# A two-layer decoder on one core: W1 units set between the K tile pairs of the pass before, and every middle pair taken by seven products

## Chip, cores and metric

The kernel runs on one core of one Trainium2 chip. The metric is device time in microseconds of one execution, as the median over several runs. Everything is float32 at the interface; TensorE works on float32 values that are cut into a high and a low part (fp32r), three matmuls for each product.

## The reference, cut to what matters

256 tokens of width 2048 go through two layers. Layer 0 is a gated short convolution, layer 1 is latent attention; each is followed by a DeepNorm and by the same kind of MLP, which is the part that the change touches:

```python
def sq_relu_mlp(x, w1, w2):
    return jnp.square(jax.nn.relu(x @ w1)) @ w2
...
h = layer_norm(ALPHA * h + sq_relu_mlp(h, mlp_w1[layer], mlp_w2[layer]),
               ln_g[layer, 1], ln_b[layer, 1])
```

w1 is 2048 by 8192 and w2 is 8192 by 2048, for each of the two layers.

## The kernel before, in words

**Passes and units.** The hidden width 8192 is cut into NQ = 8 passes of QC = 8 chunks of 128 columns. In pass q each chunk is one *W1 unit*: 16 K tiles of the input, and for each a 512-wide matmul with the high part of the weights over the high and low parts of the 256 tokens (`high`, L215) and a 256-wide one with the low part of the weights (`low`, L219), into one PSUM bank (`mm_run`, `products`). A unit is then evacuated (`whole`, L355 and L356), goes through Relu and Square on ScalarE (L718, L719), and is cut into high and low parts. The 256 columns of two neighbouring chunks and the matching rows of w2 make a *K tile pair* of the second product.

**The second product.** Pass 0 and pass 7 use plain `down`. The six passes between (`FAST`) add to running sums. In each, the four output blocks of 512 columns are taken as two groups g of two blocks. A pair can be taken *by seven products* (Strassen's scheme in Winograd's form, `fast_products`): sums and differences of the four activation quarters (S1 to S4, made by `form`) and of the four weight quarters (T1 to T4, made on the fly in `prepare`) give seven 128 by 128 by 512 products in place of eight. Each product is a `dot`, three 512-wide matmuls (L300, L302, L303). The seven running sums live in seven PSUM banks while they are added to; between uses they are parked in SBUF (in `acc` and `sums`) by copies on ScalarE. `MIXED = "sssp"` says that group 1 takes three pairs by seven products and the fourth pair plainly, by eight dots; group 0 takes all four by seven. One dot of the plain pair (`EVEN`) has its middle matmul cut in two.

**Order of the work.** In a middle pass the eight W1 units come first, back to back, on four banks in turn (`busy`); `resume` brings the parked sums of group 1 back while they run. Then `down_pairs` takes the four pairs of group 1, parks its sums, brings back those of group 0, takes its four pairs and parks or adds those. The first unit of a stretch has its third K tile `TURNED`: low before high.

**Weights.** All weights come in one `stream` in the order of use, 512 KB a load, through SyncE's DMA queue into RAW = 5 raw buffers. `prepare` cuts each into high (ScalarE cast, L127) and low (VectorE subtraction, L128); a pair for seven products is two loads and adds L162, L166, L169 and a third and a fourth cut. There are WA = 8 buffers each for high and low parts. `take` hands out the next prepared weights and emits the preparation of those up to LOOK = 5 pieces further on. The order on each engine's queue is fixed when the program is built, by the order in which the instructions are emitted and by when they are expected to be ready.

**Other work beside.** In pass 7 of the first MLP, `begin` subtracts a mean from the 16 chunks of the residual for the next norm; in passes 1 to 4 of the second MLP, `extra` adds the turned residual to one block each; in pass 7 `fold` adds the seven sums together, for both groups at once with 1024-wide VectorE instructions (L676).

Of the kernel before, what the change touches and what calls it, by code (L numbers as in the profile page):

```python
# [10 lines left out]
F32 = mybir.dt.float32  # L11
# [5 lines left out]
P = 128  # L17
# [5 lines left out]
NQ = 8  # L23
# [14 lines left out]
MIXED = "sssp"  # L38
EVEN = (QC - 1, "22")
# [14 lines left out]
def trunk(ctx: ExitStack, tc: tile.TileContext, xT, vecs, lead, w_first, w_in, w_out, w_kv, w_q, w_uk, w_uv,  # L54
# [27 lines left out]

    def mlp_stream(l):
        out = []
        for q in range(NQ):
            out += halves(w1[l, q * QC:(q + 1) * QC])
            if q not in FAST:
                out += halves(w2[l, q])
                continue
            for j, kind in enumerate(MIXED):  # L90
                out += [(w2f[l, q, 1, j, 0], w2f[l, q, 1, j, 1])] if kind == "s" else \
                    halves(w2[l, q, 2, j]) + halves(w2[l, q, 3, j])
            out += [(w2f[l, q, 0, j, 0], w2f[l, q, 0, j, 1]) for j in range(QC // 2)]
        return out
# [210 lines left out]
    def held(x, t):  # L305

        return [x[:, o + t * P:o + (t + 1) * P] for o in (0, T)]
# [35 lines left out]
    def fast_products(ps, x, forms, j, fresh, ready, onto=()):  # L343

        b, = take(1)
        a = {"11": held(x[2 * j], 0), "12": held(x[2 * j + 1], 0), "22": held(x[2 * j + 1], 1)}
        for i in range(4):
            a[f"S{i + 1}"] = [forms[:, j, o, i * P:(i + 1) * P] for o in range(2)]
        for p, l, r in FACTORS:
            dot(ps[p], b[r], a[l], p in fresh, p in ready, onto=p in onto)  # L350
# [224 lines left out]
    def mlp(idx, ln, blocks, fast, begin=None, extra=None, last=False):  # L575
# [27 lines left out]
        def place(p, g):  # L603

            return sums[:, OWN.index(p), g, :] if p in OWN else \
                block(*{"2": (2 * g, 0), "3": (2 * g + 1, 0), "4": (2 * g, 1), "22": (2 * g + 1, 1)}[p])

        def resumed(p, g, name, bank):

            ps = psum(name, bank)  # L610
            if q != FAST[0] or p not in OWN:
                nc.scalar.copy(ps, place(p, g))
            return ps
# [4 lines left out]
        def keep(p, g, ps):  # L618

            at = place(p, g)  # L620
            if q == FAST[0] and p in OWN:
                nc.scalar.copy(at, ps)
            else:
                nc.vector.tensor_tensor(at, at, ps, ALU.add)

        def resume(busy, free, ps, m):

            b2, b3, b4, b6 = free
            b1, b5, b7, b22 = busy
            for p, bank in {3: (("3", b3),), 4: (("2", b2),), 5: (("4", b4), ("1", b1)), 6: (("6", b6), ("5", b5)),  # L630
                            7: (("7", b7), ("22", b22))}.get(m, ()):
                ps[p] = resumed(p, 1, f"ps_r{p}", bank)

        def down_pairs(h, forms, busy, free, ps):

            b2, b3, b4, b6 = free
            b1, b5, b7, b22 = busy
            new = set(OWN) if q == FAST[0] else set()
            onto = set(ps) - new
            for j, kind in enumerate(MIXED):  # L640
                if kind == "s":
                    last = j == MIXED.rindex("s")
                    fast_products(ps, h, forms, j, new if j == 0 else (), OWN if last else (), onto)
                    if last:
                        for p in OWN:
                            put_back(p, 1, ps[p])
                        then = {p: resumed(p, 0, f"ps_f{p}", bank) for p, bank in (("3", b1), ("1", b5))}
                    continue
                for two in (((0, "2"), (1, "4")), ((1, "22"), (0, "3"))):
                    w, = take(1, LOOK + 1)  # L650
                    for t, p in two:
                        for kk in range(2):
                            k = 2 * j + kk
                            dot(ps[p], wide_rows(w, kk), held(h[k], t), False, k == QC - 1, (k, p) == EVEN, True)
                    if j == len(MIXED) - 1:
                        if "5" not in then:
                            then.update({p: resumed(p, 0, f"ps_f{p}", bank) for p, bank in (("5", b7), ("7", b6))})
                        for _, p in two:
                            put_back(p, 1, ps[p])
            n = QC // 2  # L660
            onto = set(then) - new
            then.update({p: psum(f"ps_f{p}", bank) for p, bank in (("2", b2), ("6", b4), ("4", b22))})
            for j in range(n):
                fast_products(then, h, forms, j, set(then) - onto if j == 0 else (), then if j == n - 1 else (), onto)
            for p, _, _ in FACTORS:
                (put_back if p in onto or p in new else keep)(p, 0, then[p])
            return (b3, b1, b5, b7), (b6, b2, b4, b22)

        def fold():

            s1, s5, s7, s6 = (sums[:, i] for i in range(4))
            c = acc.rearrange("p t (g b c) -> p t b g c", g=2, b=2)
            for d, a, b in ((c[:, 0, 0], c[:, 0, 0], s1), (s6, s6, s1), (c[:, 0, 1], c[:, 0, 1], s6), (s7, s7, s6),
                            (c[:, 1, 0], c[:, 1, 0], s7), (c[:, 1, 1], c[:, 1, 1], s7),
                            (c[:, 0, 1], c[:, 0, 1], s5), (c[:, 1, 1], c[:, 1, 1], s5)):
                nc.vector.tensor_tensor(d, a, b, ALU.add)  # L676
                yield
# [8 lines left out]
        busy, free = (0, 1, 2, 3), (4, 5, 6, 7)  # L686
        for q in range(NQ):
            ht = act.tile([P, QC, 2 * T], F32R, tag="c", name=f"h{idx}_{q}")
            h = [ht[:, k, :] for k in range(QC)]
            forms = None  # L690
            if q in FAST:
                forms = act.tile([P, QC // 2, 2, 4 * P], F32R, tag="a2", name=f"forms{idx}_{q}")
            pair = []

            def pair_tile(m):

                if m % 2 == 0:
                    pool = (act, "ab") if m % 4 else (fast, "fp")
                    t = pool[0].tile([P, 2 * T], F32, tag=pool[1], name="fp")
                    pair.append(t.rearrange("p (i t) -> p i t", i=2))  # L700
                return pair[-1]

            def form(j):
                (a11, a21), (a12, a22) = ((pair[j][:, i, :P], pair[j][:, i, P:]) for i in range(2))
                sf = fast.tile([P, 4, P], F32, tag="sf", name="sf")
                s1, s2, s3, s4 = (sf[:, i, :] for i in range(4))
                nc.vector.tensor_tensor(s1, a21, a22, ALU.add)
                nc.vector.tensor_tensor(s3, a21, a11, ALU.subtract)
                nc.vector.tensor_tensor(s2, s1, a11, ALU.subtract)
                nc.vector.tensor_tensor(s4, a12, s2, ALU.subtract)  # L710
                split(forms[:, j, 0, :], forms[:, j, 1, :], sf.rearrange("p i c -> p (i c)"))

            def hidden(m, ps, evac, *func):
                both = pair_tile(m) if q in FAST else None
                f = both[:, m % 2, :] if both is not None else tmp.tile([P, T], F32, tag="fh", name="fh", bufs=3)
                evac(ps, f, *func)
                if not func:
                    nc.scalar.activation(f, f, AF.Relu)  # L718
                nc.scalar.activation(f, f, AF.Square)  # L719
                if both is None:  # L720
                    put_split(h[m], f)
                elif m % 2:
                    at = ht[:, m - 1:m + 1, :]
                    split(at[:, :, :T], at[:, :, T:], both)
                    form(m // 2)

            if q == 0:
                for m in range(QC):
                    if m < GROUP:
                        if m == 0:  # L730
                            ws = ln.ws if ln.ws else group_of(GROUP)
                            if not ln.ws:
                                mm_wide(ws, ln.xd)
                            ln.finish()
                        ps = ws[m][1]
                    else:
                        ws = [(take(), psum("ps_w"))]
                        mm_wide(ws, ln.xd)
                        ps = ws[0][1]
                    hidden(m, ps, ln.weighted, AF.Relu)  # L740
                acc = act.tile([P, 2, D], F32, tag="a1", name=f"acc{idx}")
            else:
                folds = fold()
                begun = {}
                for m, ps in enumerate(products(QC, xhl, TURNED, busy)):
                    hidden(m, ps, whole)
                    if extra and m == 0 and q <= NB:
                        for t in range(2):
                            extra(block, q - 1, t, busy[2 + t])
# [438 lines left out]
```

## Time and profile before

| what | value |
|---|---|
| median of 3 runs (lowest, highest) | 2000.58 us (2000.33, 2001.18) |
| the profiled execution's span, first to last instruction | 1994.9 us |
| around it: the median less this span | 5.7 us |
| granted TensorE clock, mean | 1.000 |
| DMA, mean over the span | 193 GB/s |

The profile is of one execution. It gives no time for that execution beside its span, so the last row sets the span against the median of the runs; a forecast is made on the span and carried over with that difference. The span is measured from the first to the last instruction. [...]

### The profile page before, as it was taken

What the parts mean: (1) busy time and instruction counts of PE and PEld (TensorE: products, weight loads), DVE (VectorE), ACT (ScalarE), POOL (GpSimd) and SP (SyncE); (2) the same over time, 40 slices, a digit from 0 to 9 for tenths busy, and PEclk for the clock granted to TensorE, in tenths of its full rate; (3) what the DMA queues carried; (4) which work ended last, traced back from release to release, by engine and by line L of the source; (5) the groups of instructions that cost most, each with busy time, mean ns of one, the idle gap of its engine ahead of it and who ended that gap; (6) DMA issues with size and microseconds to landing.
All of it is one profiled execution on the core that took longest, in us unless ns stands there. A gap on an engine that the chain in (4) does not pass through costs nothing.

```text
span 1994.9 us, 30180 instructions
## 1 busy us (share of the span) xinstructions
PE 1987.7 (100%) x11110; PEld 1737.2 (87%) x11110; DVE 1709.4 (86%) x2555; ACT 1354.9 (68%) x2154; POOL 2.3 (0%) x21
## 2 busy tenths in 40 slices
PE   9999999999999999999999999999999999999998
PEld 8888888988888888888889998898888888888886
DVE  8667667797999989989978988777899999999985
ACT  6444445586778778777756755558677787887772
POOL 0000000000000000000000000000000000000000
PEclk9999999999999999999999999999999999999999
DMA  8666666565657466574855543656464656656483
GB/s 318 205 191 187 190 190 190 179 193 157 212 170 251 148 216 221 177 243 147 281 171 159 170 140 123 201 180 195 146 233 155 232 161 220 222 178 233 150 269 130
DMA packets 106853, 385.85 MB, mean 193 GB/s; under 512 B 11857, under 2 KB 12625, under 8 KB 106449
## 3 DMA queue, kind: packets, MB, share of 16 engines
q1 hardware_dynamic: 106560, 383.79, 59.5%
q8 instruction: 87, 1.43, 0.3%
q14 instruction: 62, 0.50, 0.1%
q10 hardware_dynamic: 144, 0.13, 0.0%
HBM read 381.78 MB, written 2.10 MB: 192 GB/s over the span
## 4 chain that ended last, share of the span: by engine, by line
PE 98%; DVE 1%; ACT 1%; issue 0%; DVEq 0%; ACTq 0%
PE ps_u L215 20%; PE ps_l L215 13%; PE ps_u L219 10%; PE ps_l L219 7%; PE ps_f L300 4%; PE ps_f L303 4%; PE ps_f L302 4%; PE ps_r L303 4%; PE ps_r L302 4%; PE ps_r L300 4%; PE ps_d L300 2%; PE ps_d L302 2%; PE ps_d L303 2%; PE ps_w L249 2%; PE ps_w L248 2%; PE ps_w L247 2%
## 5 line engine op out<-in xcount | busy, mean ns | idle before, releaser
L128 DVE TENSOR_TENSOR lo<-raw,hi 128x1024 fp32r<-128x1024 f32 x710 | 861.8, 1220 | 190.6 <-ACT hi L127 119.9
L127 ACT CAST hi<-raw 128x1024 fp32r<-128x1024 f32 x710 | 741.8, 1051 | 247.4 <-PE ps_l L215 98.1
L215 PE MATMUL ps_u<-xhl,hi 128*128 128x512 f32 x1792 | 621.7, 392 | 0.0
L219 PE MATMUL ps_u<-xhl,lo 128*128 128x256 f32 x1792 | 498.2, 279 | 0.0
L215 PEld LDWEIGHTS ps_u<-xhl,hi 128*128 128x128 f32 x1792 | 334.5, 187 | 73.6 <-ACT acc L595 0.2
L219 PEld LDWEIGHTS ps_u<-xhl,lo 128*128 128x128 f32 x1792 | 338.1, 189 | 1.8
L215 PE MATMUL ps_l<-xhl_a,hi 128*128 128x512 f32 x704 | 244.1, 393 | 0.0
L219 PE MATMUL ps_l<-xhl_a,lo 128*128 128x256 f32 x704 | 195.4, 279 | 0.0
L215 PEld LDWEIGHTS ps_l<-xhl_a,hi 128*128 128x128 f32 x704 | 132.1, 188 | 29.9
L219 PEld LDWEIGHTS ps_l<-xhl_a,lo 128*128 128x128 f32 x704 | 131.9, 188 | 0.2
L127 ACT CAST hi_t<-raw_t 128x1024 fp32r<-128x1024 f32 x84 | 88.5, 1054 | 45.8 <-DVE raw_t L162 41.4
L162 DVE TENSOR_TENSOR raw_t<-raw,raw 128x1024 f32<-128x1024 f32 x84 | 102.3, 1218 | 1.8 <-DMA raw<-in_w2f_dram 1.5
L128 DVE TENSOR_TENSOR lo_t<-raw_t,hi_t 128x1024 fp32r<-128x1024 f32 x84 | 102.4, 1219 | 0.2
L718 ACT ACTIVATE fp<-fp 128x256 f32<-128x256 f32 x96 | 40.0, 416 | 63.2 <-DVE fp L356 62.6
L215 PE MATMUL ps_l<-z,hi 128*128 128x512 f32 x240 | 82.4, 391 | 0.0
L300 PE MATMUL ps_d<-hi,h 128*128 128x512 f32 x192 | 75.0, 391 | 0.0
L302 PE MATMUL ps_d<-lo,h 128*128 128x512 f32 x192 | 75.0, 390 | 0.0
L303 PE MATMUL ps_d<-hi,h 128*128 128x512 f32 x192 | 74.8, 389 | 0.0
L249 PE MATMUL ps_w<-xd,hi 128*128 128x258 f32 x256 | 72.7, 284 | 0.0
L248 PE MATMUL ps_w<-xd,lo 128*128 128x258 f32 x256 | 72.3, 282 | 0.0
L247 PE MATMUL ps_w<-xd,hi 128*128 128x258 f32 x256 | 72.3, 282 | 0.0
L215 PE MATMUL ps_l<-oT,hi 128*128 128x512 f32 x208 | 71.3, 391 | 0.0
(296 smaller groups left out, 3963.7 us busy)
## 6 DMA issues: line engine op xcount, KB each, us to landing
raw<-in_w_dram SPq DMA_DIRECT2D x344, 512.0 KB, 4.5
raw<-in_w2f_dram SPq DMA_DIRECT2D x168, 512.0 KB, 3.9
raw<-in_w_in_dram SPq DMA_DIRECT2D x88, 512.0 KB, 4.2
raw<-in_w_out_dram SPq DMA_DIRECT2D x32, 512.0 KB, 3.7
raw<-in_w_o_dram SPq DMA_DIRECT2D x32, 512.0 KB, 4.2
raw<-in_w_kv_dram SPq DMA_DIRECT2D x10, 512.0 KB, 3.7
raw<-in_w_q_dram SPq DMA_DIRECT2D x8, 512.0 KB, 4.0
raw<-in_w_uk_dram SPq DMA_DIRECT2D x8, 512.0 KB, 3.9
```

The costliest lines, as they stand in the source:

```text
L127: nc.scalar.copy(hi, src)
L128: nc.vector.tensor_tensor(lo, src, hi.bitcast(F32), ALU.subtract)
L162: nc.vector.tensor_tensor(t.rearrange(two, a=2), b12.unsqueeze(1).to_broadcast([P, 2, BW]), r1.rearrange(two, a=2), ALU.subtract)
L215: nc.tensor.matmul(ps, w[blk // 8][0][:, blk % 8, :], x, start=first, stop=False)
L219: nc.tensor.matmul(ps[:, :T], w[blk // 8][1][:, blk % 8, :], x[:, :T], start=False, stop=last)
L247: nc.tensor.matmul(ps[:, :W], hi, x[k][:, :W], start=k == 0, stop=False)
L248: nc.tensor.matmul(ps[:, :W], lo, x[k][:, :W], start=False, stop=False)
L249: nc.tensor.matmul(ps[:, :W], hi, x[k][:, W:], start=False, stop=k == NC - 1)
L300: nc.tensor.matmul(ps, x[0], w[0], start=first, stop=False, skip_group_check=onto)
L302: nc.tensor.matmul(ps[:, at], x[0], w[1][:, at], start=False, stop=False, skip_group_check=onto)
L303: nc.tensor.matmul(ps, x[1], w[0], start=False, stop=last, skip_group_check=onto)
L718: nc.scalar.activation(f, f, AF.Relu)
```

## The change

Between the first pass and the end, the units and the pairs are no longer two stretches of a pass. `steps` walks over all units of passes 1 to 7, and after unit m of pass q comes one pair of the pass that is SHIFT = 5 units behind: its eight group-and-pair combinations i = 0 to 7. The first five units (pass 1, m below 5) and the last three (pass 7, m from 5) stand alone. All 48 such pairs of an MLP are taken by seven products; `MIXED`, `EVEN` and the plain pair go. The two groups change places from pass to pass, so that a group's sums stay in their banks from the second half of one pass to the first half of the next; they are parked, and the other group's brought back, in the middle of a pass only (`i == 0` in `products_of`, there the number of the half).

A unit's evacuation now has one bank (`unit`), or two in turn for the units that stand alone. The two units of a pair write into one row `u`, with room for the four forms; Relu and Square run once over the pair; the forms are three VectorE instructions in place of four, put in the order 21, 11, 22, 12, S1, S3, S2, S4, so that one cast and one subtraction over 896 columns cut all seven factors. `take(2, LOOK + 1)` looks one piece further for a unit. `TURN` says which units have their third K tile turned: nearly all that have a pair beside them. `fold` runs group by group with 512-wide instructions. `extra` now comes after the first four units of pass 1, `begin` is spread over pass 0, the last three units and the first two blocks after them.

The diff, cut to its core:

```diff
-MIXED = "sssp"
-EVEN = (QC - 1, "22")
+SHIFT = 5
+
+
+def TURN(q, m):
+    return m == 0 or not (q == 1 and m < SHIFT or q == NQ - 1 and m > SHIFT)
...
+    def steps():
+
+        for q in range(1, NQ):
+            for m in range(QC):
+                p, i = (q, m - SHIFT) if m >= SHIFT else (q - 1, m + QC - SHIFT)
+                yield q, m, (p, i // NB, i % NB, (p % 2) ^ (i // NB)) if p in FAST else None
+
     def mlp_stream(l):
...
+        out = halves(w1[l, :QC]) + halves(w2[l, 0])
+        for q, m, pair in steps():
+            out += halves(w1[l, q * QC + m])
+            if pair:
+                p, i, j, g = pair
+                out.append((w2f[l, p, g, j, 0], w2f[l, p, g, j, 1]))
+        return out + halves(w2[l, NQ - 1])
...
-    def fast_products(ps, x, forms, j, fresh, ready, onto=()):
+    LEFT = ("11", "22", "12", "S1", "S3", "S2", "S4")
+
+    def fast_products(ps, x, j, fresh, ready, onto=()):
 
         b, = take(1)
...
+        a = {n: [x[j // 2][:, j % 2, o, i * P:(i + 1) * P] for o in range(2)] for i, n in enumerate(LEFT)}
         for p, l, r in FACTORS:
             dot(ps[p], b[r], a[l], p in fresh, p in ready, onto=p in onto)
...
+        def form(u):
+
+            a21, a11, a12, s1, s2, s4 = (u[:, i * P:(i + 1) * P] for i in (0, 1, 3, 4, 6, 7))
+            two = u.rearrange("p (i c) -> p i c", c=P)
+            nc.vector.tensor_tensor(s1, a21, u[:, 2 * P:3 * P], ALU.add)
+            nc.vector.tensor_tensor(two[:, 5:7, :], two[:, 0:5:4, :], a11.unsqueeze(1).to_broadcast([P, 2, P]),
+                                    ALU.subtract)
+            nc.vector.tensor_tensor(s4, a12, s2, ALU.subtract)
+
+        def finish_pair(j, u):
+            f = factors[j // 2][:, j % 2]
             if q in FAST:
...
+                form(u)
+                split(f[:, 0, :], f[:, 1, :], u[:, P:])
+            else:
+                split(f[:, 0, :2 * T], f[:, 1, :2 * T], u[:, :2 * T])
...
+        base = Banks.count
+        bank = {p: (base + i) % 8 for i, p in enumerate(("6", "unit", "3", "1", "5", "7", "2", "4"))}
...
+        def products_of(p, i, j, g):
+
+            nonlocal folds
+            order = [f[0] for f in FACTORS]
+            end = i == 0 or p == FAST[-1]
+            fast_products(ps, factors, j, set(fresh), order if j == NB - 1 and end else (), onto)
+            fresh.clear()
+            if j == NB - 1 and end:
+                begun[g] = 0
+                for o in order:
+                    put_back(o, g, ps[o])
+                    if i == 0:
+                        resume(o, 1 - g)
+            if p == FAST[-1] and j == NB - 1:
+                folds = chain(folds, fold(g))
+
+        for q, m, pair in steps():
+            lone = pair is None
+            if q == FAST[0] and m == SHIFT:
+                for o, _, _ in FACTORS:
+                    resume(o, 1)
+            w = take(2, LOOK + 1)
+            at = "6" if lone and m % 2 == 0 else "unit"
+            un = psum("ps_u", bank[at])
+            mm_run([(w, un)], xhl, 0, NC, NC, turned=TURNED if TURN(q, m) else None)
+            if m % 2 == 0:
+                u = fast.tile([P, 8 * P], F32, tag="fp", name="fp")
+            whole(un, u[:, (m % 2) * T:(m % 2 + 1) * T])
+            if m % 2:
+                for function in (AF.Relu, AF.Square):
+                    nc.scalar.activation(u[:, :2 * T], u[:, :2 * T], function)
+                if m > 1 or lone:
+                    finish_pair(m // 2, u)
...
+            if pair:
+                products_of(*pair)
+            if m == 1 and not lone:
+                finish_pair(0, u)
```

More of the change, by code (lines that the diff above doesn't have):

```diff
@@ L305, in held @@
     def held(x, t):
+        if len(x.shape) == 3:
+            return [x[:, o, t * P:(t + 1) * P] for o in range(2)]
         return [x[:, o + t * P:o + (t + 1) * P] for o in (0, T)]
@@ L605, in place @@
             return sums[:, OWN.index(p), g, :] if p in OWN else \
[L606 to L613, printed above, removed]
+                block(*{"2": (2 * g, 1), "3": (2 * g + 1, 1), "4": (2 * g, 0)}[p])
         def put_back(p, g, ps):
             nc.scalar.copy(place(p, g), ps)
[L618 to L675, printed above, removed]
+        def fold(g):
+            s1, s5, s7, s6 = (sums[:, i, g, :] for i in range(4))
+            c = [[block(2 * g + b, t) for b in range(2)] for t in range(2)]
+            for d, a, b in ((c[1][0], c[1][0], s1), (s6, s6, s1), (c[1][1], c[1][1], s6), (s7, s7, s6),
+                            (c[0][0], c[0][0], s7), (c[0][1], c[0][1], s7), (c[1][1], c[1][1], s5), (c[0][1], c[0][1], s5)):
@@ L684, in last_sum @@
             nc.scalar.copy(finals[n, t], block(n, t))
[L686 to L690, printed above, removed]
-            if q in FAST:
[L692 to L737, printed above, removed]
@@ L740, in mlp @@
-                    hidden(m, ps, ln.weighted, AF.Relu)
-                acc = act.tile([P, 2, D], F32, tag="a1", name=f"acc{idx}")
-            else:
[L743 to L749, printed above, removed]
-                    if q in FAST:
-                        resume(busy, free, begun, m)
-                    if q == NQ - 1:
-                        next(folds, None)
-                        if last and m >= QC - 2:
-                            for t in range(2):
-                                last_sum(m - QC + 2, t, free[2 * (m - QC + 2) + t])
-                        if begin:
-                            begin(range(max(2 * m, 1), 2 * m + 2))
@@ L760, in mlp @@
-            if q == NQ - 1 and last:
-                for i, (n, t) in enumerate(((2, 0), (3, 0), (2, 1), (3, 1))):
-                    last_sum(n, t, busy[i])
-                blocks(block, finals, h)
-                return
-            if q == NQ - 1:
-                blocks(block, put, h)
-                return
-            if q == 0:
-                for n in range(NB):
-                    down(h, put, n)
-                    if begin and n == 1:
-                        begin(range(1))
-            else:
-                busy, free = down_pairs(h, forms, busy, free, begun)
+                    ln.finish()
@@ new lines, in mlp @@
+                ps = ws[m][1]
+            else:
+                ws = [(take(), psum("ps_w"))]
+                mm_wide(ws, ln.xd)
+                ps = ws[0][1]
+            f = tmp.tile([P, T], F32, tag="fh", name="fh", bufs=3)
+            ln.weighted(ps, f, AF.Relu)
+            nc.scalar.activation(f, f, AF.Square)
+            put_split(h[m], f)
+        acc = act.tile([P, 2, D], F32, tag="a1", name=f"acc{idx}")
+        for n in range(NB):
+            down(h, put, n)
+            if begin and n == 1:
+                begin(range(1), (Banks.count + 4) % 8)
@@ new lines, in mlp, with resume @@
+        base = Banks.count
+        bank = {p: (base + i) % 8 for i, p in enumerate(("6", "unit", "3", "1", "5", "7", "2", "4"))}
+        spare = [bank[p] for p in ("3", "1", "5", "7", "2", "4", "6", "unit")]
+        factors = [act.tile([P, QC // 4, 2, 7 * P], F32R, tag=tag, name=f"h{idx}{tag}") for tag in ("c", "a2")]
+        ps, onto, fresh = {}, set(), set()
+        folds = iter(())
+        def resume(p, g, at=None):
+            ps[p] = psum(f"ps_{p}", bank[at or p])
+            onto.discard(p)
+            if p in OWN and begun[g] == FAST[0]:
+                fresh.add(p)
+            else:
+                nc.scalar.copy(ps[p], place(p, g))
+                onto.add(p)
@@ L776, in to_wide @@
+        for _ in folds:
+            pass
+        h = [factors[j // 2][:, j % 2, :, i * T:(i + 1) * T] for j in range(QC // 2) for i in range(2)]
+        if last:
+            for i, (n, t) in enumerate(((2, 0), (3, 0), (2, 1), (3, 1))):
+                last_sum(n, t, spare[4 + i])
+            blocks(block, finals, h)
+            return
+        Banks.count = base + 2
+        blocks(block, put, h)
     def to_wide(block, put, h):
@@ L788, in to_wide @@
             down(h, put, n)
+            if n < 2:
+                prepare_chunks(range(10 + 3 * n, 13 + 3 * n))
             if n:
```

38 lines of the change are left out of this document (21 added, 17 removed).

## Prediction, made before the changed kernel was run

> **What bounds the kernel now.** First the page's top, then the list of waits of TensorE.
>
> ```profile
> span 1994.9 us, 30180 instructions
> PE 1987.7 (100%) x11110; PEld 1737.2 (87%) x11110; DVE 1709.4 (86%) x2555; ACT 1354.9 (68%) x2154; POOL 2.3 (0%) x21
> ```
> ```profile
> PE ps_e L1075 <- ACT umeans L1073: 1.6, 1, 1.6
> PE warm L372 <- DVE col L373: 1.0, 1, 1.0
> PE ps_f L300 <- ACT acc L616: 0.5, 1, 0.5
> ```
>
> TensorE is busy for 1987.7 of 1994.9 us, and all its waits come to 3.1 us: one at each end of the program, one in the middle. So the time is what TensorE's instructions need, and a change pays only by taking matmuls away or setting them closer, as long as the other engines keep up. How near they are is seen in the busy time by pass, from one turned unit to the next (columns: stretch, length, PE, PEld, DVE and ACT busy with instruction counts), and below it in the second product of one pass.
>
> ```profile
> core 0: us, PE busy (x) PEld busy (x) DVE busy (x) ACT busy (x) POOL busy (x), PEclk, DMA share, GB/s
> 537.22:620.45 83.23, 83.23 (x429) 71.28 (x429) 78.12 (x102) 66.70 (x104) 0.00 (x0) 1.00 0.61 199
> 620.45:703.67 83.22, 83.22 (x429) 71.27 (x429) 80.15 (x103) 66.35 (x102) 0.00 (x0) 1.00 0.63 207
> 870.12:954.28 84.16, 83.70 (x430) 71.13 (x429) 79.04 (x103) 66.28 (x102) 0.00 (x0) 1.00 0.59 199
> ```
> ```profile
> 664.81:680.90 16.09, 16.09 (x73) 13.30 (x72) 15.95 (x21) 13.06 (x21) 0.00 (x0) 1.00 0.47 141
> 680.90:686.40 5.50, 5.50 (x27) 4.58 (x26) 5.50 (x6) 5.50 (x10) 0.00 (x0) 1.00 0.40 162
> 686.40:703.67 17.27, 17.27 (x79) 14.37 (x78) 17.09 (x20) 12.23 (x17) 0.00 (x0) 1.00 0.68 210
> ```
>
> VectorE is the second bound, and a close one: 80.15 of 83.22 us in a whole pass, 38.54 of 38.86 us (99%) in the pairs, and still TensorE waits for nothing there, because the weights prepared beside the units carry it. Only the last middle pass of the first MLP is longer, by 0.9 us.
>
> **TensorE's own time.** The chain of work gives a pass from one turned pair of matmuls to the next; the timeline gives the pieces (start, duration, instruction).
>
> ```profile
> 453.75 0.47 PE ps_u L215 x2
> 869.88 0.47 PE ps_u L215 x2
> ```
> ```profile
> 454.88 0.39 PE L215 MATMUL ps_u<-xhl,hi 128*128 128x512 f32 x1
> 487.12 0.39 PE L215 MATMUL ps_u<-xhl,hi 128*128 128x512 f32 x1
> 501.06 0.39 PE L303 MATMUL ps_r<-hi,forms 128*128 128x512 f32 x1
> 514.89 0.39 PE L300 MATMUL ps_r<-hi,h 128*128 128x512 f32 x1
> 497.17 0.39 PE L300 MATMUL ps_r<-hi,forms 128*128 128x512 f32 x1
> 499.48 0.39 PE L302 MATMUL ps_r<-lo_t,forms 128*128 128x512 f32 x1
> 536.00 0.39 PE L215 MATMUL ps_u<-xhl,hi 128*128 128x512 f32 x1
> 537.76 0.39 PE L215 MATMUL ps_u<-xhl,hi 128*128 128x512 f32 x1
> ```
>
> Five passes lie between the first two rows: 416.13 / 5 = 83.23 us each. Between rows 3 and 4 (454.88 and 487.12) lie 93 pairs of a high and a low matmul: 0.3467 us a pair, 5.547 us a unit. Between 501.06 and 514.89 lie 61 matmuls of dots: 0.2267 us each. The two kinds do not follow each other for nothing: the first ten matmuls of the dots after a unit take 2.31 us where ten settled ones take 2.27, so 0.04 more; the first five pairs of a turned unit after dots take 1.76 us where five settled pairs take 1.73, so 0.03 more. Eight units (44.38) and 57 dots (171 matmuls, 38.77) make 83.15, and the 0.08 left pays both borders and the cut matmul of `EVEN`. The rows are rounded to 0.01, so I take 0.06 for the two borders.
>
> [...] The rows show 226.7 ns, and more at borders. [...]
>
> **The change, part by part.** *Seven for eight.* Of a middle pass, one dot goes: 3 x 0.2267 = 0.68 us, and the split of `EVEN`. *Borders.* A pass had one of each kind; now every step has both, eight a pass. A step is a unit, 21 matmuls and two borders: 5.547 + 4.761 + 0.06 = 10.37 us, a pass of eight 82.95 us against 83.23. That is 0.28 us a pass, 3.4 us for twelve passes. The dots alone would give 8.2 us; seven more borders of each kind a pass take 7 x 0.06 x 12 = 5.0 us of it back, and the split of `EVEN` gives some 0.2 us. *The late pass.* In the pass that took 84.16 us, the chain leaves TensorE:
>
> ```profile
> 936.91 0.52 ACT t L127
> 937.43 0.49 ACT acc L616
> 937.97 0.50 PE ps_f L300
> ```
>
> A product waited until ScalarE had parked the old sum of its bank (0.49 us a copy, L616), behind casts. Now a whole unit, 5.55 us, lies between the parking and the next use, so I count these 0.9 us as gone. *Parking.* Once a pass, seven sums go out and seven come in on ScalarE, 14 copies of 0.49 us, 6.9 us, where the code before asked for 23 or 24. A sum is final every three matmuls (0.68 us), so the copies are done some 8 us after the pair's start; the next pair starts after 10.37 us and wants the last sum 4 us later still. Hidden; with the cover gone at most 2 us a swap, twelve swaps. Behind these copies on ScalarE's queue stand the casts of the next weights, thus VectorE: it may stand idle for some 3 us a swap, out of what it is ahead.
>
> *VectorE.* The start-to-start times come from the chain of waits of a stretch where it is the chain:
>
> ```profile
> 914.09 0.28 DVE sf L708
> 914.38 1.14 DVE raw_t L162
> 915.52 1.14 DVE lo L128
> 916.65 0.60 DVE raw L166
> 917.26 0.33 DVE fp L356
> ```
>
> A step has six 1024-wide instructions (two for the unit, four for the pair: 6.84 us), three 512-wide (1.80) and one evacuation (0.33). Every second step has the forms: 0.28 + 0.33 + 0.28 and a cut of 896 columns, which no row has; between 0.60 (512) and 1.14 (1024), by width 1.00. Half of 1.89 is 0.95. Sum 9.92 us of 10.37, 79.4 us a pass, no more than the 80.15 that the trace carries without a wait, though now even over the pass and no longer 99% in one half. ScalarE loses about ten copies a pass and gains 1.5 us of casts; no bound. *Loads.* The pair in place of the plain one is two loads as before; bytes are the same, at 207 GB/s in the pass shown.
>
> *A single bank for units.* A unit may start when the one before it is evacuated (a ScalarE copy, then L356); the pair gives 4.8 us for it, where four banks gave three units. Nothing if VectorE is on time; behind a late L356 stand the forms and the next weights, and TensorE waits for it. *Forms.* In an odd step VectorE waits twice for ScalarE, unless other work is set between: for Relu and Square (no row at 512 wide; 0.49 us each by the copy above) and for a cast of 896 columns (0.52 us at 512, thus 0.9 by width), 1.9 us together. The trace before shows that it is:
>
> ```profile
> 470.43 0.29 DVE L710 TENSOR_TENSOR sf<-fp,sf 128x128 f32<-128x128 f32 x1
> 470.64 1.22 DVE L128 TENSOR_TENSOR lo<-raw,hi 128x1024 fp32r<-128x1024 f32 x1
> 471.78 0.69 DVE L128 TENSOR_TENSOR forms<-sf,forms 128x512 fp32r<-128x512 f32 x1
> ```
>
> A weight's subtraction stands between the last form and its cut. I take these waits as filled. *Edges.* `extra`, `begin` and `fold` move the same elements; `fold` as sixteen 512-wide (9.6 us) for eight 1024-wide (9.1 us) beside pass 7, four steps of which have 1.2 us more on VectorE (11.1 of 10.37): 3 us out of its lead. For all new small waits together I put 0.3 us; bounds 0 and 2.
>
> **The sum.** 1994.9 - 3.4 - 0.9 + 0.3 = 1990.9 us of span; with the 5.7 us to the median, **1996.6 us**. A measurement of this kernel can tell about 0.2% from no change (4.0 us), so the bound to "faster" is 1996.6: the forecast stands on it. Its own range is 1994.5 to 1999.
>
> **Rivals.** *1. Borders cost nothing.* If the settled rates hold at once, only the dots count: 36 matmuls fewer, 8.2 us, and the 0.9: 1994.9 - 9.1 + 5.7 = 1991.5 us. Against it stand the rows at 497.17 and 536.00; for it, that they may come from waits which the rows do not show, and that the new order has other ones. Chance: 11%.
>
> *2. Units stay in a slower rhythm.* An unturned unit of the stretch before the first MLP shows one:
>
> ```profile
> 273.42 0.39 PE L215 MATMUL ps_u<-z,hi 128*128 128x512 f32 x1
> 278.71 0.40 PE L215 MATMUL ps_l<-z,hi 128*128 128x512 f32 x1
> ```
>
> 15 pairs in 5.29 us, 0.3527 each, 0.096 us more a unit. With 53 matmuls a step, odd, and only 13 settled dots ahead of a unit, half or all of 96 units could fall into it: 4.6 or 9.2 us, 2001.2 or 2005.8. Against it: each turned unit after dots settles at 0.3467 within five pairs. Chance: 12%.
>
> *3. VectorE becomes the bound, and it is slower.* One mechanism: the waits of an odd step that aren't filled. VectorE has 10.37 - 9.92 = 0.45 us a step to spare; it decides from 0.9 us unfilled in each odd step on. All 1.9 us unfilled give 0.50 us a step, 96 steps, 48 us: 2045. With 1.2 us, 0.15 a step, 14 us: 2011 us, which I take. Against it: in the pass from 620.45 VectorE had only 3.07 us without work. For it: there the units ran ahead of a slack stretch, and now no stretch is slack; the lead is one step of eight buffers. [...] Chance of this rival: 25%.
>
> **How the numbers follow.** Forecast 52%, split by the bound: 29 faster, 23 same. Rival 1: 11 faster. Rival 2: 8 same, 4 slower. Rival 3: 5 same, 20 slower. Faster 40%, same 36%, slower 24%. The range takes in rival 1 and most of rival 2 and ends near the taken price of rival 3: 1991.5 to 2010; left out are about half of rival 3 and the lower part of rival 1.
>
> **What would show it.** Right: steps of 10.37 us on TensorE in both MLPs, 1008 matmuls of dots in each one's middle passes, no wait of TensorE beyond a few tenths, VectorE near 79 us in eight steps. Borders: first ten matmuls of each pair at 2.31 us; if 2.27, rival 1. A pair of high and low at 0.353 in the units: rival 2. Waits of units for L356 or of products for L128, steps of 10.5 us and more with VectorE at 99%: rival 3; waits for L612 would be the parking.

## The result, and the profile after

The changed kernel takes 2022.01 us (median of 4 runs, 2019.67 to 2024.11) where the kernel before takes 2000.53 (4 runs): a ratio of 1.0113, 95% interval 1.0099 to 1.0127. It is slower by 21.5 us; the forecast was 4 us faster, and the time lies above the range. The profiled execution took 2019.67 us and has a span of 2017.9.

The top of its page, and the longest waits of TensorE (engine, tile and line that waited, what it waited for, us in total, times, longest):

```profile
span 2017.9 us, 29768 instructions
PE 1992.8 (99%) x11062; PEld 1730.8 (86%) x11062; DVE 1721.9 (85%) x2493; ACT 1299.6 (64%) x1914; POOL 2.3 (0%) x21
```
```profile
PE ps L308 <- DVE lo L134: 6.3, 8, 1.9
PE ps L306 <- ACT h3a L133: 3.7, 2, 3.4
PE ps L306 <- ACT h1a L133: 3.4, 1, 3.4
PE ps L306 <- ACT hi_t L133: 3.1, 6, 1.2
```

Before, all waits came to 3.1 us. Now 16.5 us stand in these four rows alone, all in the middle of the MLPs: products (L306, L308) wait for weights (hi_t, lo) and for forms (h1a, h3a). This list counts only what the engine sat idle. From start to start (a 512-wide matmul's row lasts 0.39 us, and the next one starts 0.23 us after it), the 48 steps with a pair take 509.9 and 511.4 us in the two MLPs, where 48 steps of 10.37 are 497.8: 12.1 and 13.6 us are lost. Does VectorE lack the time? The busy time of two passes says no (columns as before: stretch, length, PE, PEld, DVE, ACT):

```profile
620.92:706.56 85.64, 83.90 (x429) 71.15 (x428) 78.51 (x95) 59.58 (x81) 0.00 (x0) 1.00 0.60 195
706.56:791.31 84.75, 84.12 (x428) 70.71 (x427) 79.83 (x97) 60.98 (x83) 0.00 (x0) 1.00 0.62 199
```

VectorE works 78.5 and 79.8 us a pass, as forecast (79.4), but a pass now lasts 84.75 to 85.64 us, so VectorE idles for 5 to 7 us of it. What it and ScalarE wait for is new; first the changed kernel's waits for the loads of pairs, then those of the kernel before:

```profile
ACT hi L133 <- DMA raw<-in_w2f_dram: 72.0, 60, 2.3
DVE raw_t L168 <- DMA raw<-in_w2f_dram: 27.8, 16, 4.1
```
```profile
ACT hi L127 <- DMA raw<-in_w2f_dram: 13.4, 14, 1.5
DVE raw_t L162 <- DMA raw<-in_w2f_dram: 1.5, 5, 0.6
```

100 us of waits for the pairs' loads stand against 15. (For the other weights of the MLPs, `in_w_dram`, it is the other way round: ScalarE waits 8.0 us against 29.9.) Yet the DMA engines are busy for only 60% of those passes, and a pair's load lands 3.9 us after its issue in both kernels (the median on their pages): the loads are not slow, they are *issued late*. The timeline of a step without a swap shows why (start, duration, engine, instruction; SPq is SyncE's DMA queue, a row with x2 there holds both loads of a pair):

```profile
674.81 1.47 SPq L144 DMA_DIRECT2D raw<-in_w2f_dram  x2
...
678.59 1.05 ACT L133 CAST hi<-raw 128x1024 fp32r<-128x1024 f32 x1 [1.93 <-DMA raw<-in_w2f_dram]
...
679.67 1.22 DVE L134 TENSOR_TENSOR lo<-raw,hi 128x1024 fp32r<-128x1024 f32 x1 [0.88 <-ACT hi L133]
...
681.15 1.22 DVE L168 TENSOR_TENSOR raw_t<-raw,raw 128x1024 f32<-128x1024 f32 x1
...
684.15 1.22 DVE L134 TENSOR_TENSOR lo_t<-raw_t,hi_t 128x1024 fp32r<-128x1024 f32 x1
...
685.39 1.66 SPq L144 DMA_DIRECT2D raw<-in_w2f_dram  x2
```

The first load of a pair is issued at 674.81. ScalarE waits for it until 678.59, and VectorE waits for that cast until 679.67. Then VectorE makes the pair's sum (`raw_t`) and later reads it for the last time, for its low part (`lo_t`), until 684.15 + 1.22 = 685.37. At 685.39 the next pair's first load is issued; in 83 of the 94 pairs that follow another it is issued within 0.04 us of that reading's end, so it takes the buffer that the sum leaves. That is a closed loop: 3.8 us from issue to cast, 6.8 us of cast and VectorE's work, 10.58 us in a step of 10.37. The next turn, to 695.79, takes 10.40; six turns from 632.95 on take 10.47 each, and five behind the next swap (719.48 to 771.07) 10.32. So the loop holds the step and leaves next to nothing with which to make up a delay. Five buffers serve five uses a step: the two loads of a unit, the two of a pair, and the pair's sum, which takes a raw buffer without being a load.

The swap of the sums brings such a delay. In this stretch of the same timeline, the casts for the unit's weights stand behind the copies of the swap on ScalarE, and the pair's second load was issued at 696.92 (the second of the two that start at 695.79):

```profile
695.79 1.46 SPq L144 DMA_DIRECT2D raw<-in_w2f_dram  x2
696.82 0.68 DVE L134 TENSOR_TENSOR t<-raw,t 128x512 fp32r<-128x512 f32 x1
...
699.63 0.61 ACT L692 COPY ps<-acc 128x512 f32<-128x512 f32 x1
700.15 2.97 ACT L133 CAST hi<-raw 128x1024 fp32r<-128x1024 f32 x3
701.14 1.23 DVE L168 TENSOR_TENSOR raw_t<-raw,raw 128x1024 f32<-128x1024 f32 x1 [3.64 <-DMA raw<-in_w2f_dram]
...
705.83 0.50 PE L308 MATMUL ps<-lo,h1c 128*128 128x512 f32 x1 [1.74 <-DVE lo L134]
```

VectorE has nothing from 697.5 to 701.14: the sum waits for the load, and the unit's subtractions, which fill that time in other steps, have no casts. Three microseconds later TensorE waits.

The two longest pauses, 3.4 us each, begin with a late load too, as rows of the first MLP show: a cast waits 2.01 us for a pair's load, the sum and all behind it are late, the next `hi_t` waits 2.82 us for its sum, and the form's cast stands behind it in ScalarE's queue.

```profile
589.84 1.05 ACT L133 CAST hi<-raw 128x1024 fp32r<-128x1024 f32 x1 [2.01 <-DMA raw<-in_w2f_dram]
...
603.53 1.04 ACT L133 CAST hi_t<-raw_t 128x1024 fp32r<-128x1024 f32 x1 [2.82 <-DVE raw_t L168]
604.48 0.93 ACT L133 CAST h1a<-fp 128x896 fp32r<-128x896 f32 x1
605.47 0.50 PE L306 MATMUL ps<-hi,h1a 128*128 128x512 f32 x1 [3.36 <-ACT h1a L133]
```

### The profile page after: what moved, and what is told of

Read it like the earlier page. It is cut to its first block, busy times and chain, and to the rows that moved or that the text cites. A ratio compares the mean times of both kernels' runs of the same rounds, so it can differ in the third digit from the quotient of the medians.

```text
span 2017.9 us, 29768 instructions
## 1 busy us (share of the span) xinstructions
PE 1992.8 (99%) x11062; PEld 1730.8 (86%) x11062; DVE 1721.9 (85%) x2493; ACT 1299.6 (64%) x1914; POOL 2.3 (0%) x21
## 4 chain that ended last, share of the span: by engine, by line
PE 65%; DVE 17%; DMA 8%; ACT 6%; issue 4%; DVEq 0%; ACTq 0%
PE ps_l L221 13%; PE ps_u L221 8%; DMA raw<-in_w2f_dram 8%; PE ps_l L225 7%; DVE lo L134 5%; PE ps_u L225 4%; ACT hi L133 3%; DVE lo_t L134 3%; DVE raw_t L168 3%; PE ps L308 3%; PE ps L309 3%; PE ps L306 2%; PE ps_d L308 2%; PE ps_d L306 2%; PE ps_d L309 2%
## 5 line engine op out<-in xcount | busy, mean ns | idle before, releaser
L225 PE MATMUL ps_u<-xhl,lo 128*128 128x256 f32 x1792 | 486.0, 280 | 0.0
L133 ACT CAST hi_t<-raw_t 128x1024 fp32r<-128x1024 f32 x96 | 101.3, 1055 | 142.2 <-DVE raw_t L168 135.9
L221 PEld LDWEIGHTS ps_l<-xhl_a,hi 128*128 128x128 f32 x704 | 132.1, 188 | 29.9
L168 DVE TENSOR_TENSOR raw_t<-raw,raw 128x1024 f32<-128x1024 f32 x96 | 116.9, 1217 | 28.1 <-DMA raw<-in_w2f_dram 27.8
L134 DVE TENSOR_TENSOR lo_t<-raw_t,hi_t 128x1024 fp32r<-128x1024 f32 x96 | 116.9, 1218 | 1.3 <-ACT hi_t L133 1.2
L727 ACT ACTIVATE fp<-fp 128x512 f32<-128x512 f32 x112 | 70.8, 632 | 36.9 <-DVE fp L364 35.4
L172 DVE TENSOR_TENSOR raw<-raw,raw_t 128x512 f32<-128x512 f32 x96 | 66.0, 688 | 1.7
L175 DVE TENSOR_TENSOR raw<-raw 128x512 f32<-128x512 f32 x96 | 66.0, 687 | 1.5
L134 DVE TENSOR_TENSOR t<-raw,t 128x512 fp32r<-128x512 f32 x96 | 65.6, 683 | 1.7 <-ACT t L133 1.6
```

The costliest lines, as they stand in the source:

```text
L133: nc.scalar.copy(hi, src)
L134: nc.vector.tensor_tensor(lo, src, hi.bitcast(F32), ALU.subtract)
L168: nc.vector.tensor_tensor(t.rearrange(two, a=2), b12.unsqueeze(1).to_broadcast([P, 2, BW]), r1.rearrange(two, a=2), ALU.subtract)
L221: nc.tensor.matmul(ps, w[blk // 8][0][:, blk % 8, :], x, start=first, stop=False)
L225: nc.tensor.matmul(ps[:, :T], w[blk // 8][1][:, blk % 8, :], x[:, :T], start=False, stop=last)
L727: nc.scalar.activation(u[:, :2 * T], u[:, :2 * T], function)
```

## The experiments

Four theories were set against each other. **A**, the parking: 14 copies at a swap hold the casts back. **B**, the raw buffers: five are too few for a pair in every step, so loads are issued late. **C**, the order written on TensorE's queue: the next pair's matmuls stand ahead of the unit and block it. **D**, VectorE's own work (rival 3 of the prediction). The kernel before, run beside them on the same chips, took 1999.23, 1999.61, 1999.88 and (one run) 1998.85 us, so that times of different experiments can be compared to about 1 us.

**No parking in four of six passes (theory A).**

```diff
-            end = i == 0 or p == FAST[-1]
+            end = i == 0 and p in (FAST[0], FAST[-1]) or p == FAST[-1]
```

> Leaves out the parking and bringing back of the sums in the middle of the passes 2 to 5 (the sums of both groups run together there). Theory A, parking: the 14 copies of a swap stand ahead of the weights' casts on ScalarE, VectorE idles 2.5 to 3.6 us at each, and TensorE pays for it. Of six swaps an MLP the four in the middle go, and most of the 27 us of TensorE's gaps with them: 2003 to 2008 us. Theory B, raw buffers: the loads of a pair come late whatever ScalarE does, so little changes: 2016 to 2022. Theory C, order of TensorE's matmuls: without the copies the unit's bank is seen free early, nothing of the next pair is set ahead of it, and the gaps of 1.2 to 2.2 us per pass go: 2008 to 2012.

Measured: 2009.09 us (2008.17 to 2010.03), span 2006.7. ScalarE's waits for the pairs' loads fall from 72.0 to 24.8 us. The pauses at the swaps left out are gone, the two at the forms are not:

```profile
PE ps L306 <- ACT h1a L133: 3.7, 2, 3.5
PE ps L306 <- ACT h3a L133: 3.3, 1, 3.3
```

Leaving out eight of the twelve swaps takes back 12.9 us, 1.6 us a swap, of the 21.5. Parking is no whole cause.

**TensorE's queue in program order (theory C).**

```diff
+            unit_end = mm_run([(w, un)], xhl, 0, NC, NC, turned=TURNED if TURN(q, m) else None)
...
-                products_of(*pair)
+                with tc.issue_after(unit_end.ins):
+                    products_of(*pair)
```

> The matmuls of a pair may not be set ahead of the unit before it; nothing else is changed. Theory C: the gaps at the matmuls of the next pair that stand ahead of a unit (about 1.2 to 2.2 us in each of eight passes) go: 2008 to 2012 us. Theories A and B: VectorE delivers the weights no earlier, the same wait is found a unit later or at the unit itself: 2018 to 2024, or a little more.

Measured: 2028.91 us (2026.2 to 2030.11). The waits did not go; they moved to the unit, which now waits for the evacuation of the one before:

```profile
PE ps_u L221 <- DVE fp L365: 16.4, 10, 2.4
```

Theory C falls. The time is 6.9 us longer, so pulling the next pair's matmuls ahead had filled part of the waits.

**The swap spread over two steps (theory A again, with no work left out).**

```diff
-                for o in order:
-                    put_back(o, g, ps[o])
-                    if i == 0:
-                        resume(o, 1 - g)
...
+                swap(order[:3] if i == 0 else order)
+                if i == 0:
+                    later.append(lambda: swap(order[3:]))
...
             w = take(2, LOOK + 1)
+            while later:
+                later.pop()()
```

> Of a swap's seven sums, three are parked and brought back right behind the pair, the other four only behind the look-ahead of the next unit, so that casts can go between. Theory A: VectorE's idle time at a swap falls from 2.5 to 3.6 us to about 1, TensorE's gaps by half or more: 2003 to 2012 us. Theory B: no change, 2018 to 2024. Theory C: only if the order of matmuls changes too; 2010 to 2022.

Measured: 2005.43 us (2004.81 to 2007.47; ratio to before 1.0033, 1.0021 to 1.0045). That takes 16.6 us back, though the waits for loads are still there (89.1 us):

```profile
ACT hi L133 <- DMA raw<-in_w2f_dram: 89.1, 68, 2.5
```

This points to two things that meet in a pause of TensorE: loads that come late, and a ScalarE that has no casts ready to fill VectorE's time.

**A sixth raw buffer (theory B).** The room comes from T4's second buffer, which moves to the ends of the rows of the forms; the computation is the same.

```diff
-RAW, WA = 5, 8
+RAW, WA = 6, 8
...
```

> Six raw buffers for the weights in place of five; the room comes from the fourth difference's second buffer, which moves into the free ends of the rows that hold the factors. Theory B: ScalarE's waits for loads of pairs (72 us in all, 60 times) and VectorE's (28 us) fall to a third, VectorE gets the 2 us a pass back that it idles in even steps, and TensorE's gaps fall by 15 us or more: 2003 to 2010 us. Theory A alone: the idle time at the swaps stays, 2014 to 2022. Theory C: 2015 to 2022.

Measured: **1993.80 us** (7 runs, 1993.45 to 1994.22), ratio to before 0.9973 (0.9961 to 0.9984): 0.3% faster than the kernel before, and 28.2 us faster than the changed one. First its page, then all its listed waits of TensorE and VectorE's wait for the pairs' loads, then a pass; then two loads of a pair, the last reading of the sum before and this pair's sum in the timeline:

```profile
span 1992.4 us, 29754 instructions
```
```profile
PE ps_e L1065 <- ACT umeans L1063: 1.6, 1, 1.6
PE warm L385 <- DVE col L386: 1.1, 1, 1.1
```
```profile
DVE raw_t L168 <- DMA raw<-in_w2f_dram: 12.3, 7, 2.1
```
```profile
702.90:785.90 83.00, 83.00 (x426) 70.65 (x425) 79.80 (x96) 60.70 (x83) 0.00 (x0) 1.00 0.62 204
```
```profile
642.50 5.52 SPq L144 DMA_DIRECT2D raw<-in_w2f_dram  x2
...
646.45 1.22 DVE L134 TENSOR_TENSOR lo_t<-raw_t,hi_t 128x1024 fp32r<-128x1024 f32 x1
...
652.73 1.22 DVE L168 TENSOR_TENSOR raw_t<-raw,raw 128x1024 f32<-128x1024 f32 x1
```

Only the two waits at the ends of the program are left. VectorE has the same 79.80 us of work and now does it within 83.00 us. The first load of a pair is issued at 642.50, 5.2 us before the last reading of the sum ends (646.45 + 1.22 = 647.67); the second load (647.69) is the one that follows it. Waits of ScalarE for a pair's load are gone from its list, where they came to 72.0 us. VectorE starts the sum of this pair 5.5 us into its step (its unit began at 647.26), where the changed kernel started the same one 8.3 us into it (660.17, unit at 651.87); for the pair before it is 7.0 against 8.5. So the buffer bought VectorE 1.5 to 3 us of lead. It still waits 2 us for a load at the swaps, but pays swaps and forms out of that lead. Theory B holds as the sufficient cause, and A's copies cost TensorE nothing once it is mended. The orders of the engines' queues are settled anew with each build; what share of the 28.2 us comes from another order was not separated. The kernel before was not run with six buffers; its 3.1 us of TensorE's waits leave it little to gain.

**Fewer raw buffers, in the changed kernel and in the one before.**

```diff
-RAW, WA = 5, 8
+RAW, WA = 4, 8
```

> The changed kernel with four raw buffers in place of five. Theory B (the pair's two loads and their sum hold raw buffers through all of VectorE's work on the pair, so loads are issued late): a sixth buffer gave 25.5 us of span, so a fourth in place of the fifth costs at least as much again, 2045 or more, with ScalarE's casts waiting for loads in the first place of its waits. Theory A (ScalarE's parking alone) or D (VectorE's load alone): no loads late, so about 2022, within 5 us.

> The kernel before with four raw buffers in place of five, as a control for the run beside it. If the need for raw buffers comes with the interleaving (a pair in every step, and no stretch in which loads get ahead), the old order loses clearly less than the changed kernel does: 0 to 15 us, 2000 to 2015. If raw buffers are as scarce in the old order, it loses as much: 2025 or more.

Measured: 2186.05 us for the changed kernel (one run) and 2085.34 for the kernel before (one run). The first is what B asks for, with more waits for the pairs' loads (72.0 us with five buffers):

```profile
ACT hi L133 <- DMA raw<-in_w2f_dram: 105.4, 82, 3.0
```

The control missed: I expected 0 to 15 us and it lost 86. Raw buffers were scarce in the old order too; it stood right above its own cliff (four 2085, five 2000). The interleaving needs one more to stand clear of it: four 2186, five 2022, six 1994.

**The same memory dealt out otherwise.** Four buffers for loads, one for the sum alone.

```diff
-RAW, WA = 5, 8
+RAW, WA = 4, 8
...
-        t = raws.tile([P, 1024], F32, tag="raw", name=f"raw{i}_t")
+        t = raws.tile([P, 1024], F32, tag="sum", name=f"raw{i}_t", bufs=1)
```

> The changed kernel's memory of five raw buffers dealt out otherwise: four for loads, the fifth for the pair's sum (raw_t) alone. In the changed kernel a step asks the ring of five for five uses: four loads and the sum, which no load fills. If the sum's place in the ring is what holds loads back, its own buffer frees them: 1995 to 2010. If the count of buffers is what is short (theory B by the count: four loads a step through four buffers, each of which must be free again within a step of 10.37 us while the sum's buffer stands idle for most of it), it is no better than the changed kernel and rather worse: 2022 to 2060.

Measured: 2069.85 us (one run), somewhat above the upper end. Taking the sum out of the ring does not help when the loads then have four buffers only; sharing the five is the better deal by 48 us. This speaks for the count as what is short.

**Less work on VectorE (theory D).**

```diff
-        nc.vector.tensor_tensor(b12, b22, t[:, :BW], ALU.subtract)
...
-        nc.vector.tensor_tensor(t4, b21, b12, ALU.subtract)
```

> The changed kernel, five raw buffers, without two of the weights' differences (T1's and T4's 512-wide subtractions on VectorE are left out, so their products take the wrong weights): 1.2 us a step less on VectorE, 8.7 of 10.37 us. Theory D (VectorE's work itself is what is late): every wait goes, 1993.8. Theory B (raw buffers held through the pair's work, late loads): the buffers are held some 1.2 us shorter of a hold that spans more than a step, so part of the waits goes, between 1997 and 2012, and ScalarE still waits for loads of pairs.

Measured: 2009.41 us (2007.03 to 2010.71). VectorE is busy for 69.49 us of 82.90 (first fence) and still waits for loads (second):

```profile
620.00:702.90 82.90, 82.15 (x420) 69.57 (x419) 69.49 (x79) 61.17 (x82) 0.00 (x0) 1.00 0.64 199
```
```profile
DVE raw_t L168 <- DMA raw<-in_w2f_dram: 80.8, 55, 3.3
```

Taking an eighth of VectorE's work away gains 12.6 us, where one buffer gains 28.2 with all of the work. D is not the cause; VectorE's work matters as a link of the loop (both instructions left out stand between the sum and its last reading).

**All pairs by seven products in the old order.** What the interleaving is good for.

```diff
-MIXED = "sssp"
+MIXED = "ssss"
...
```

> The kernel before with its own order (eight units, then the pairs of both groups) and only the plain pair and its cut matmul replaced: all eight pairs of a middle pass by seven products. If TensorE's matmuls alone set the time, twelve dots of 0.68 us and the cuts go: 8.2 us less, about 1992. If VectorE sets the pairs (38.54 of 38.86 us before), the replaced pair asks it for 6.36 us in place of 2.28, some 4 us a pass more in a stage with 0.3 us to spare and 0.7 us shorter: 12 x 4 us = 48 us more, less 8, about 2040. I expect the second; then the interleaving has a use of its own, to give that VectorE work the units' time.

Measured: 2053.96 us (2050.38 to 2056.68), ratio 1.0268 (1.0253 to 1.0283). A stretch of the pairs, and TensorE's longest wait, once in each of twelve passes:

```profile
670.00:700.00 30.00, 28.88 (x127) 22.96 (x126) 29.79 (x38) 22.80 (x34) 0.00 (x0) 1.00 0.39 135
```
```profile
PE ps_f L300 <- ACT hi_t L127: 16.2, 12, 1.7
```

VectorE at 29.79 of 30.00 us bounds the pairs. The seven products alone cost 54 us; the interleaving gives their VectorE work the units' time.

**Units between pairs not turned (rival 2 of the prediction), six buffers.**

```diff
-    return m == 0 or not (q == 1 and m < SHIFT or q == NQ - 1 and m > SHIFT)
+    return q == 1 and m == 0
...
```

> The changed kernel with six raw buffers, and only the first unit of a stretch (pass 1, unit 0) with low before high in its third K tile; the units between pairs are not turned. Rival 2 of the prediction had a slower rhythm of 0.3527 us a pair of high and low, 0.096 us a unit: some 49 units an MLP change, 9.4 us in all, 2003 against 1993.8. If the settled rhythm does not depend on the turn once dots stand ahead of every unit, 1993.8 as before; if only every second unit falls into it (53 matmuls a step are odd), about 1998.5.

Measured: 1999.29 us (10 runs, 1998.57 to 1999.6), 5.5 above the turned one. Starts of two neighbouring units, first here and then in the turned kernel with six buffers:

```profile
616.90 0.39 PE L226 MATMUL ps_u<-xhl,hi 128*128 128x512 f32 x1
...
627.33 0.39 PE L226 MATMUL ps_u<-xhl,hi 128*128 128x512 f32 x1
```
```profile
626.53 0.39 PE L226 MATMUL ps_u<-xhl,hi 128*128 128x512 f32 x1
...
636.89 0.39 PE L226 MATMUL ps_u<-xhl,hi 128*128 128x512 f32 x1
```

A step is 10.43 us against 10.36. The time is near the number for every second unit; spread over 98 units, 5.5 us are 0.06 us each (an estimate), where 0.096 was expected. Whether all of them lose a little or some of them more, and how much of it lies at the border ahead of a unit, was not shown.

**Six buffers and the spread swap together.**

> Six raw buffers and the swap of the sums spread over two steps (three swapped at once, four behind the next unit's look-ahead): the two edits that helped alone, together. Theory B (the raw buffers are the whole cause, and the parking matters only because it makes loads later still): with six buffers no wait of TensorE is left, so spreading adds nothing, 1993.8 within 1 us. If parking has a cost of its own (theory A), some 1 to 3 us less, 1991 to 1993.

Measured: 2003.55 us (11 runs, 2002.87 to 2003.87), 9.8 *slower* than six buffers alone. Neither theory had this. TensorE's waits, and one of these places:

```profile
PE ps L311 <- ACT h3a L133: 4.0, 4, 1.1
PE ps L311 <- ACT h1a L133: 4.0, 4, 1.1
```
```profile
1714.48 1.05 ACT L133 CAST hi_t<-raw_t 128x1024 fp32r<-128x1024 f32 x1 [3.03 <-DVE raw_t L168]
1715.43 0.93 ACT L133 CAST h3a<-fp 128x896 fp32r<-128x896 f32 x1
...
1716.42 0.50 PE L311 MATMUL ps<-hi,h3a 128*128 128x512 f32 x1 [1.09 <-ACT h3a L133]
```

Eight waits of up to 1.1 us: the form's cast now stands behind a `hi_t` that itself waits 3.03 us for its sum. In the kernel with six buffers alone the same cast stands ahead of it. The order is fixed when the program is built, and moving the copies reshuffled it. Why it chose so was not tried further.

**The kernel before, profiled again.**

> The kernel before, unchanged: a second profiled execution with its own time beside its span. In every run of the changed kernel and of the experiments the time is 1.8 us above the span, where the forecast carried 5.7 us from the median to the span of before. If the profiled execution of before was a short one, this span lies at 1996 to 2000 and the time 1.8 us above; if the kernel before has a different surround, the span is 1995 again and the time 5.7 us above.

Measured: 1998.07 us with a span of 1996.3, thus 1.8 us around the span.

## Why the prediction was wrong, point by point

- **The step that failed is *Loads*:** "The pair in place of the plain one is two loads as before; bytes are the same". Both are so, and neither is what limits. A pair for seven products takes three raw buffers, one of them for its sum, and the next pair's first load is not issued before VectorE has read that sum for the last time. With such a pair in every step, one turn of this loop takes 10.2 to 10.6 us where a step has 10.37. The prediction put no wait on it. One more buffer takes 25.5 us off the span (2017.9 to 1992.4).
- ***Parking*, "hidden".** The sizes were right: VectorE idles for some 3 us a swap (3.64 in the row), and TensorE lost 1.6 us a swap, within the 2 that the prediction gave for the cover gone. But "out of what it is ahead" took a lead for granted that the loads no longer allow; without the copies of eight swaps 12.9 us go, with a sixth buffer their cost is nil.
- ***Forms*, taken as filled.** With late loads they are not: two pauses of 3.4 us. With six buffers they are, as forecast. The 0.3 us for all new waits, bounds 0 and 2, was the term that was mis-sized, by some 25 us.
- ***VectorE*.** 79.4 us a pass forecast, 78.5 and 79.8 measured in the two passes shown. That the trace carried 80.15 did not mean that it would carry 79.4 in another order.
- **TensorE's own time** was right: with six buffers a step takes 10.36 us (626.53 to 636.89) where 10.37 was worked out, both borders paid, so rival 1 falls. With six buffers the span is 1992.4 against the 1990.9 worked out; those 1.5 us lie within the bounds given for small waits and were not traced further. *The late pass*' 0.9 us are gone there.
- **Rival 2** did not come, because the units are turned; the run without turning shows that unturned units do take longer, 5.5 us in all.
- **Rival 3** came nearest in time (2011) with the wrong mechanism: VectorE has time to spare in the pass and waits for loads. Its condition, VectorE at 99%, is not seen; with 10 us a pass less work, 2009 us remain.
- **The 5.7 us** from span to median were not a surround: every execution that shows both has 1.8 us. Before's profiled execution was some 4 us shorter than the median of its runs. Against the kernel before run beside it, six buffers save 5.4 us, where the sum gave 4.0.

## What to carry to other kernels

When work that was done in blocks is interleaved, count for each buffer pool the uses per step and the loop of issue, landing and last reading, and set it against the step; bytes per second and busy shares do not show it. A share of idle time on an engine is a lead only if its inputs can be there early: before calling a delay hidden, find how early the next load *can* be issued. A kernel that stands at the edge of such a loop pays for every small delay, so look at the pool first and at the delays afterwards.

## What the runs showed of the hardware

After some pauses TensorE ran at about half its rate for a while; the mean granted clock is between 0.993 and 0.999 in eight of the profiled executions and 1.000 in the others. In the changed kernel, after a pause of 1.86 us and (last two rows) behind the one at 605.47, of 3.36:

```profile
1661.64 0.64 PE L308 MATMUL ps<-lo,h3c 128*128 128x512 f32 x1 [1.86 <-DVE lo L134]
1662.08 0.63 PE L309 MATMUL ps<-hi,h3c 128*128 128x512 f32 x1
...
605.81 0.40 PE L308 MATMUL ps<-lo,h1a 128*128 128x512 f32 x1
606.05 0.40 PE L306 MATMUL ps<-hi,h1a 128*128 128x512 f32 x1
```

Behind the first, starts of 512-wide matmuls lie some 0.43 us apart, and the trace's granted clock is 0.50 from 1661.84 to 1665.25, for 3.41 us; by these two numbers that costs 1.7 us more than the pause, an estimate. Behind the second, longer one they lie 0.23 to 0.24 apart after one of 0.34, and the granted clock stays at 1.00. So the length of a pause is not all that decides: 1.86 us brought the half rate and 3.36 us did not. Nor does the longest wait of a run tell: in the listed waits of TensorE it is 1.7 us both with all pairs by seven in the old order, at a mean clock of 0.997, and with the swap spread over two steps, at 1.000. What else decides was not shown.
